# A transformer trunk on one core: where the weight halves, the last pool and some small tiles lie in SBUF, and the order of two groups of small matmuls

## The chip, the core and the metric

The kernel runs on one core of a Trainium2 chip. Its engines run side by side, each through its own queue of instructions: TensorE (PE in the profile; its weight loads are PEld), VectorE (DVE), ScalarE (ACT), GpSimd (POOL) and SyncE (SP), the last of which only issues DMAs here. The metric is the device time of one execution in microseconds (us), and the median of several runs is compared. One core alone is used, so no core waits for another.

## The reference

One layer over a sequence of 256 positions and 2048 channels, all in float32. Cut to what matters:

```python
h = rms_norm(x, norm_g)
proj = h @ w_in                                   # 2048 x 24576
a_qkv, a_gate, b_in, b_gate, c_qkv, c_gate, merge = split(proj)
# A: 3 groups of dilated windowed attention, 8 heads of 128, combined by their denominators
# B: width-3 convolution, then two long FFT convolutions with implicit filters
# C: differential attention, 8 heads, two softmax maps per head, RMSNorm per head
branches = [A * silu(a_gate), B * silu(b_gate), C * silu(c_gate)]
proj_b = einsum('bsnw,nwd->bsnd', branches, w_proj)   # 3 x 1024 x 2048
y = sum(sigmoid(merge + merge_b) * proj_b)
out = rms_norm(x + y @ w_out, final_g)
```

## The kernel before

**The stream of weights.** All weights (`w_in`, `w_proj`, `w_out`) are cut on the host into `NU` = 232 units of 1 MB, [128, 2048] float32 each, in the order in which they are used (`_plan`, L34). Unit i is loaded by SyncE into one of three `raw` buffers (`load`, L167). Each half of a unit (1024 columns) is then split into a high part, rounded to the matmul's short float format (`fp32r`), and the remainder: ScalarE casts the high part (L180), VectorE subtracts (L181). The result is the tile `hl[i, h]`, [128, 2, 1024], with the high part first and the low part 4096 bytes behind it, in four buffers that take turns.

**How a unit is multiplied** (`mm_unit`, L717). A product of two split operands is taken as three matmuls, high·high, high·low and low·high. Two layouts are used.

- Layout b (gates, conv, q and k): the weight half is the stationary operand, 128 columns at a time, and the activations stream: L740 streams 512 elements (high and low activations side by side), L742 streams 256 with the low weight. A half has eight such pairs. In units 0 to 15 the activations are the tiles `xg`, later `hT`.
- Layout a (v, merge, proj, out): the activations are stationary, and the weight half streams in pieces of 512: L761, L762 and L763, 24 matmuls in a unit. The activations are `hT` for v and merge, `bhl` (the split output of a branch) for proj, `yhl` (the split merged output) for out. Every matmul has a weight load of its own, also where two follow each other with the same stationary operand.

**Where tiles lie.** A tile's place is its byte address in each partition. The pools give addresses in the order of allocation, so one tile of odd size moves all that follow. Pieces of `hl`, `hT`, `xg`, `bhl` and `yhl` start at whole multiples of 512 bytes from their tile's start, so a tile's place modulo 512 is that of all its pieces. The built program has:

| tiles | pool or tag | place modulo 512 before |
|---|---|---|
| `hl` (both halves of all units) | `base`, tag `hl` | 288 |
| `hT` | `base` | 288 |
| `xg`, `bhl0`, `bhl2`, `yhl1` to `yhl3`, `qka`, `qkb`, `va`, `vb`, `cv` | `base`, tag `slab` | 256 |
| `bhl1`, `yhl0` | last pool `n`, tag `slab2` | 480 |
| `hidHL`, `dftHL`, `idftHL` (tables of branch B) | `base` | 352 |
| work tiles of branches A and B (`PTh`, `ef`, `vh`, `zh` ...) | pool `ab` | 480 |

**What sets the order.** The program is written out unit by unit (L1009 to L1106): for unit i, the results of unit i-1 are taken out of PSUM, unit i+1 is split, unit i+3 is loaded, and unit i is multiplied in two halves. Between the two halves of a unit stands at most one step of each of two task queues, "a" (attention) and "b" (the rest). Each step issues a short group of other matmuls and the work of VectorE and ScalarE on it. So PE alternates: a half of a unit, a group of small matmuls, a half, and so on. The groups that matter here:

- `t_attn_a` (L525), for each of eight heads: the logits `lg` (twice `mm3`, three matmuls of split operands at L385 to L387, each with 256 elements, and four plain float32 matmuls at L533, each of which PE runs as two passes); one unit later the transposes `pt` (L560, L563); one unit later the product `av` (`mm3`, eight float32 matmuls at L577, `mm3`).
- the forward transforms `ps_f` (L385 to L387, twelve matmuls) and the filters `ps_ef` (L438) of branch B.
- once, in unit 8: `stats_rstd` (L311, two transposes L314, then `std` on ScalarE and `rstd` on VectorE) and `strip_products` (L246, two float32 matmuls L250).

Ahead of everything, 14 float32 matmuls on a tile of ones (L242) run while the first loads are under way. The same tile gives one column to the norm of branch C (L666).

Small tiles (`mx`, `sm`, `rc`, `cmx`, `csm`, `crc`, `ms`, `lam_e`, `tot`, `ss`, `st`, `diff_g`) are allocated where they are first used.

Of the kernel before, what the change touches and what calls it, by code (L numbers as in the profile page):

```python
# [10 lines left out]
F32 = mybir.dt.float32  # L11
F32R = mybir.dt.float32r
# [66 lines left out]
UNITS = _plan()  # L79
# [77 lines left out]
def trunk_kernel(ctx: ExitStack, tc: tile.TileContext, A, out, dbg=None):  # L157
    nc = tc.nc
# [4 lines left out]
    phase = {}  # L163
# [3 lines left out]
    def load(i):  # L167
        if i < NU:
            raw[i] = base.tile([128, 2048], F32, name=f"raw{i}", tag="raw", bufs=3)
            n = 2 if i == 1 else 1  # L170
            for h in range(n):
                c = slice(2048 // n * h, 2048 // n * (h + 1))
                nc.sync.dma_start(raw[i][:, c], A["ws"][i][:, c])

    def split_part(i, h, c):
        if (i, h) not in hl:
            hl[i, h] = base.tile([128, 2, 1024], F32R, name=f"hl{i}_{h}", tag="hl", bufs=4)
        t = hl[i, h][:, :, c]
        src = raw[i][:, 1024 * h:1024 * h + 1024][:, c]
        nc.scalar.copy(t[:, 0], src)  # L180
        nc.vector.tensor_tensor(t[:, 1], src, t[:, 0].bitcast(F32), op=OP.subtract)  # L181
# [11 lines left out]
    def k4(name, shape, dt=F32):  # L193
        return phase["ab"].tile(shape, dt, name=name, tag="k4", bufs=6)
# [43 lines left out]
    tabl = const("tabl", [35, 32])  # L238

    wps = psum.tile([128, 128], F32, name="wps", tag="pa")  # L240
    for j in range(14):
        nc.tensor.matmul(wps, ones, ones, start=j == 0, stop=j == 13)  # L242
    wide_acc = psum.tile([128, 2, 512], F32, name="acc4", tag="pb")
# [13 lines left out]
    dft = slab("dft", [128, 4, 128])  # L257
    idft = base.tile([128, 4, 128], F32, name="idft", tag="i2")
    convw = const("convw", [128, 24, 3])
    diff_g = const("diff_g", [128, 1])  # L260

# [5 lines left out]

    convraw = []
    for j in range(2):
        t = base.tile([128, 260], F32, name=f"convraw{j}")  # L270
        nc.vector.memset(t[:, 0:1], 0.0)
        nc.vector.memset(t[:, 258:260], 0.0)
        convraw.append(t)

# [33 lines left out]

    tot = base.tile([128, 2], F32, name="tot")

# [214 lines left out]
    def t_attn_a(h):  # L525
# [4 lines left out]
        for qt in range(2):  # L530
            mm3(lg[:, qt, 0:256], q(qk, 0, qt), q(qk, 1, qt), qk[:, 2], qk[:, 3], True, True)
            for g in (1, 2):
                nc.tensor.matmul(lg[:, qt, 128 + 128 * g:256 + 128 * g], q(qk2, 2 * g - 2, qt),  # L533
                                 q(qk2, 2 * g - 1, qt), start=True, stop=True)
        P = k4(f"P{h}", [128, 2, 512])
        mx = base.tile([128, 2], F32, name=f"mx{h}", tag="mx", bufs=2)
        sm = base.tile([128, 2], F32, name=f"sm{h}", tag="sm", bufs=2)
        for qt in range(2):
# [3 lines left out]
            else:  # L542
# [6 lines left out]
                                 accum_out=sm[:, qt:qt + 1])  # L549
        rc = base.tile([128, 2], F32, name=f"rc{h}", tag="rc", bufs=2)  # L550
        nc.vector.reciprocal(rc, sm)
# [41 lines left out]
    def lam_init():  # L593
        lamp = k1("lamp").rearrange("p (a d) -> p a d", a=4)
        nc.gpsimd.dma_start(lamp, bass.AP(tensor=A["lamp"].tensor, offset=A["lamp"].offset,
                                          ap=[[0, 128], [64, 4], [1, 64]]))
        pr = k1("lam_p")
        prv = pr[:, 0:128].rearrange("p (a d) -> p a d", a=2)
        lv = lamp.rearrange("p (a b) d -> p a b d", a=2)
        nc.vector.tensor_tensor(prv, lv[:, :, 0], lv[:, :, 1], op=OP.mult)  # L600
        e = base.tile([128, 2], F32, name="lam_e")
        nc.vector.tensor_reduce(e, prv, axis=mybir.AxisListType.X, op=OP.add)
        nc.scalar.activation(e, e, AF.Exp)
        nc.vector.scalar_tensor_tensor(nlam, e[:, 1:2], -(0.8 - 0.6 * math.exp(0.0)), e[:, 0:1],
                                       op0=OP.add, op1=OP.subtract)

    def t_attn_c(h):
# [8 lines left out]
        P = phase["c"].tile([128, 2, 2, 256], F32, name=f"cP{h}", tag="cP", bufs=1)  # L616
        mx = base.tile([128, 4], F32, name=f"cmx{h}", tag="cmx", bufs=2)
        sm = base.tile([128, 4], F32, name=f"csm{h}", tag="csm", bufs=2)
        for qt in range(2):
            bias = cb[:, 1 - qt:3 - qt].rearrange("p s j -> p (s j)")  # L620
            for m in range(2):
# [5 lines left out]
                                     accum_out=sm[:, j:j + 1])  # L627
        rc = base.tile([128, 2, 2], F32, name=f"crc{h}", tag="crc", bufs=2)
        nc.vector.reciprocal(rc, sm.rearrange("p (a b) -> p a b", a=2))
# [27 lines left out]
    def t_cnorm():  # L657
        co = CO["o"]
        ms = base.tile([128, 16], F32, name="ms")
        ps = psum.tile([128, 16], F32, name="ps_ms", tag="pb")  # L660
        prev = None
        for hp in range(5):
            if prev is not None:
                for j in range(4):
                    c = 4 * (hp - 1) + j
                    nc.tensor.matmul(ps[:, c:c + 1], prev[:, j // 2, 128 * (j % 2):128 * (j % 2) + 128],  # L666
                                     ones[:, 0:1], start=True, stop=True)
# [49 lines left out]
    def mm_unit(i, h, ms=(0, 1)):  # L717
        u = UNITS[i]
        t = hl[i, h]
        if i < NS:  # L720
# [288 lines left out]
    for i in range(NU):  # L1009
        if i == i_conv:  # L1010
            load_abias(0)
            load_abias(1)
# [10 lines left out]
        if i == i_n[0] + 18:  # L1023
            drain("a")
            c_ctx.close()
            phase["n"] = n_ctx.enter_context(tc.tile_pool(name="n", bufs=1))
            tasks["b"].append(t_bsplit(1, slab2))
        if i == i_n[1] + 10:
            tasks["b"].append(t_bsplit(2, slab))
        if i == i_out:  # L1030
            for m in range(2):
                xres.append([])
                for j in range(2):
                    t = slab2(f"xres{m}_{j}", [128, 1024])
                    nc.gpsimd.dma_start(t, A["x"][m][:, 1024 * j:1024 * j + 1024])
                    xres[m].append(t)
                fin.setdefault("ss", []).append(base.tile([128, 4], F32, name=f"ss{m}"))
            fin["g"] = []
# [70 lines left out]
    for m in range(2):  # L1109
        st = base.tile([128, 4], F32, name=f"st{m}")  # L1110
        nc.vector.tensor_reduce(st[:, 0:1], fin["ss"][m][:, 0:3], axis=mybir.AxisListType.X, op=OP.add)
# [69 lines left out]
```

## Time and profile before

| | |
|---|---|
| median of 3 runs | 1413.57 us (1412.72 to 1414.65) |
| the profiled execution | 1414.19 us, of which 1412.4 us are the span from the first to the last instruction |
| matmuls and weight loads in it | 7382 each |
| granted TensorE clock | 0.999 of full |
| HBM read | 262.07 MB, 187 GB/s over the span |

How to read it: an instruction is named by its line, engine, operation and tiles, as out<-in without buffer numbers. Matmuls overlap in the records: a matmul of 512 elements is shown with some 0.39 us, yet the next one starts after 0.23 us. What a matmul costs in a dense stream is therefore the distance from one start to the next, not its shown length. The view of windows gives, for a stretch of time, how many instructions of each engine fall in it; a stretch divided by its weight loads is that distance. PE's count in a window has one or two more, since those under way at the edges are counted too.

### The profile page before, as it was taken

How to read it: one execution, taken by the hardware profiler on the slowest of the kernel's cores; microseconds unless marked ns; L12 is line 12 of the kernel's file. 1: busy time of each engine (PE TensorE's matmuls, PEld its weight loads, DVE VectorE, ACT ScalarE, POOL GpSimd, SP SyncE). 2: the span in 40 equal slices, each digit the busy share in tenths (PEclk: the TensorE clock that was granted, in tenths of full speed). 3: DMA queues.
4: the chain of work that ended last, by engine and by line, in shares of the span. 5: the costliest groups of instructions: out<-in, count | busy, mean ns of one | idle time of the engine just before them, and what ended most of it. 6: DMA issues, size and time to landing. Idle time of an engine off the chain costs nothing.

```text
span 1412.4 us, 18607 instructions
## 1 busy us (share of the span) xinstructions
PE 1401.9 (99%) x7382; PEld 1199.7 (85%) x7382; DVE 917.2 (65%) x1245; ACT 702.8 (50%) x1019; POOL 48.7 (3%) x84
## 2 busy tenths in 40 slices
PE   9999999999999999999999999999999999999997
PEld 8888888888988888888888888888888888888886
DVE  5697767676767676576655677765655655555554
ACT  5665544544454444444455675764444444444443
POOL 1000000000000000000000000000000000000000
PEclk9999999999999999999999999999999999999999
DMA  9665555554555544554455555555555555557552
GB/s 343 205 206 200 180 174 173 171 185 168 161 171 185 193 164 159 168 206 150 150 192 187 177 184 173 186 186 187 186 197 205 194 209 191 200 197 276 179 204 94
DMA packets 41943, 265.47 MB, mean 188 GB/s; under 512 B 5619, under 2 KB 5630, under 8 KB 12416
## 3 DMA queue, kind: packets, MB, share of 16 engines
q1 hardware_dynamic: 35712, 246.44, 49.5%
q0 software_dynamic: 5568, 16.80, 4.4%
q8 instruction: 58, 0.95, 0.3%
q10 hardware_dynamic: 576, 1.05, 0.2%
q14 instruction: 29, 0.24, 0.0%
HBM read 262.07 MB, written 2.20 MB: 187 GB/s over the span
## 4 chain that ended last, share of the span: by engine, by line
PE 99%; DMA 0%; DVE 0%; SPq 0%; ACT 0%; issue 0%; DVEq 0%
PE acc L740 28%; PE acc L761 16%; PE acc L762 16%; PE acc L763 16%; PE acc L742 14%; PE acc L728 1%; PE acc L729 1%; PE ps_ef L438 1%; PE ps_o L504 1%; PE av L577 1%; PE lg L533 1%; DMA raw<-in_ws 0%; PE ps_fZ L385 0%; PE clg L615 0%; PE ps_fG L386 0%; PE ps_fZ L386 0%
## 5 line engine op out<-in xcount | busy, mean ns | idle before, releaser
L181 DVE TENSOR_TENSOR hl<-raw,hl 128x1024 fp32r<-128x1024 f32 (+1 forms) x465 | 560.1, 1220 | 220.7 <-ACT hl L180 217.7
L180 ACT CAST hl<-raw 128x1024 fp32r<-128x1024 f32 (+1 forms) x465 | 478.7, 1046 | 244.7 <-PE acc L763 209.6
L740 PE MATMUL acc<-hT,hl 128*128 128x512 f32 x1536 | 542.6, 397 | 0.0
L742 PE MATMUL acc<-hT,hl 128*128 128x256 f32 x1536 | 431.3, 281 | 0.0
L740 PEld LDWEIGHTS acc<-hT,hl 128*128 128x128 f32 x1536 | 288.3, 188 | 65.3 <-issue 0.3
L742 PEld LDWEIGHTS acc<-hT,hl 128*128 128x128 f32 x1536 | 291.0, 189 | 0.5
L761 PE MATMUL acc<-hl,hT 128*128 128x512 f32 x640 | 250.7, 392 | 0.0
L762 PE MATMUL acc<-hl,hT 128*128 128x512 f32 x640 | 249.6, 390 | 0.0
L763 PE MATMUL acc<-hl,hT 128*128 128x512 f32 x640 | 249.6, 390 | 0.0
L763 PEld LDWEIGHTS acc<-hl,hT 128*128 128x128 f32 x640 | 120.2, 188 | 25.0
L762 PEld LDWEIGHTS acc<-hl,hT 128*128 128x128 f32 x640 | 120.3, 188 | 24.3 <-DVE hl L181 0.2
L761 PEld LDWEIGHTS acc<-hl,hT 128*128 128x128 f32 x640 | 120.3, 188 | 24.2
L769 ACT COPY eb<-acc 128x256 f32<-128x256 f32 x80 | 29.6, 372 | 123.7 <-PE acc L742 119.8
L761 PE MATMUL acc<-hl,bhl 128*128 128x512 f32 x192 | 75.9, 395 | 0.0
L762 PE MATMUL acc<-hl,bhl 128*128 128x512 f32 x192 | 75.9, 395 | 0.0
L763 PE MATMUL acc<-hl,bhl 128*128 128x512 f32 x192 | 75.4, 393 | 0.0
L740 PE MATMUL acc<-xg,hl 128*128 128x512 f32 x160 | 56.9, 398 | 0.0
L761 PE MATMUL acc<-hl,yhl 128*128 128x512 f32 x128 | 50.6, 395 | 0.0
L762 PE MATMUL acc<-hl,yhl 128*128 128x512 f32 x128 | 50.6, 395 | 0.0
L763 PE MATMUL acc<-hl,yhl 128*128 128x512 f32 x128 | 50.4, 394 | 0.0
L742 PE MATMUL acc<-xg,hl 128*128 128x256 f32 x160 | 45.1, 282 | 0.0
L763 PEld LDWEIGHTS acc<-hl,bhl 128*128 128x128 f32 x192 | 36.0, 188 | 8.5
(314 smaller groups left out, 1328.0 us busy)
## 6 DMA issues: line engine op xcount, KB each, us to landing
raw<-in_ws SPq DMA_DIRECT2D x230, 1024.0 KB, 4.9
mb<-in_merge_b POOLq DMA_DIRECT2D x12, 256.0 KB, 3.4
xt<-in_xT SPq DMA_DIRECT2D x8, 256.0 KB, 8.0
tok<-in_x POOLq DMA_DIRECT2D x4, 512.0 KB, 10.9
w<-in_w POOLq DMA_DIRECT2D x8, 256.0 KB, 4.7
xres<-in_x POOLq DMA_DIRECT2D x4, 512.0 KB, 7.6
raw<-in_ws SPq DMA_DIRECT2D x3, 512.0 KB, 7.6
ab<-strips POOLq DMA_DIRECT2D x8, 192.0 KB, 3.5
```

What stands on the lines that cost most here:

```text
L180: nc.scalar.copy(t[:, 0], src)
L181: nc.vector.tensor_tensor(t[:, 1], src, t[:, 0].bitcast(F32), op=OP.subtract)
L438: nc.tensor.matmul(ps[:, tt], hidHL[:, 128 * tt:128 * tt + 128], wh[:, j], start=j == 0, stop=j == 1)
L504: nc.tensor.matmul(ps[:, ct, 128 * par:128 * par + 128], p[:, par, f, 128 * ct:128 * ct + 128], idft[:, 2 * par + f], start=f == 0, stop=f ...
L533: nc.tensor.matmul(lg[:, qt, 128 + 128 * g:256 + 128 * g], q(qk2, 2 * g - 2, qt), q(qk2, 2 * g - 1, qt), start=True, stop=True)
L577: nc.tensor.matmul(av[:, qt], v2[:, qt, g - 1, v0:v0 + 128], PTg[:, 2 * g - 2 + qt], start=False, stop=False)
L740: nc.tensor.matmul(acc, t[:, 0, 128 * j:128 * j + 128], m, start=first and j == 0, stop=False)
L742: nc.tensor.matmul(acc[:, 0:256], t[:, 1, 128 * j:128 * j + 128], m[:, 0:256], start=False, stop=last and j == 7)
L761: nc.tensor.matmul(o, xh, wh, start=kt == 0, stop=False)
L762: nc.tensor.matmul(o, xh, wl, start=False, stop=False)
L763: nc.tensor.matmul(o, xl, wh, start=False, stop=kt == u["kt"] - 1)
L769: nc.scalar.copy(t, acc[:, 256:512])
```

## The change

Eight edits, none of which adds or removes a matmul.

1. A tile `hl` becomes 2056 elements wide, 32 bytes more than it needs. A unit's two parts are laid from byte 0 of it or from byte 32 (`halves`): from byte 0 for the units of proj whose branch is not 1 and for the units of out with t > 0; from byte 32 for all others.
2. The four buffers of `hl` get tags of their own, and small tiles are put between them (`put`), with pads, so that each buffer starts at 256 modulo 512.
3. In the last pool, `n`, a tile of 320 bytes (`npad`) is allocated first, and a tile `pad2` of 128 bytes in `base`.
4. The small tiles are allocated once, two of a kind by turns, in the room between the buffers.
5. The tile of ones becomes two: `ones_w` [128, 128] for the matmuls ahead of everything, in a `k1` buffer, and `ones` [128, 1].
6. `convraw` is allocated ahead of `convw`.
7. In `t_attn_a` the float32 matmuls of both query tiles come first, then both `mm3`.
8. In unit 8 `strip_products` comes ahead of `stats_rstd`.

| tiles | place modulo 512 before | after |
|---|---|---|
| `hl` of proj with branch 0 or 2, and of out with t > 0 | 288 | 256 |
| all other `hl` | 288 | 288 |
| `hT` | 288 | 288 |
| `xg`, `bhl0`, `bhl2`, `yhl1` to `yhl3` and the other slabs | 256 | 256 |
| `bhl1`, `yhl0` | 480 | 288 |
| `hidHL`, `dftHL`, `idftHL` | 352 | 320 |
| work tiles in the pools of branches A, B and C | 480 | 480 |

```diff
+    def halves(i, h):
+
+        u = UNITS[i]
+        slabs = u["kind"] == "proj" and u["br"] != 1 or u["kind"] == "out" and u["t"] > 0
+        o = 0 if slabs else 8
+        return hl[i, h][:, o:o + 2048].rearrange("p (a b) -> p a b", a=2)
+
     def split_part(i, h, c):
         if (i, h) not in hl:
-            hl[i, h] = base.tile([128, 2, 1024], F32R, name=f"hl{i}_{h}", tag="hl", bufs=4)
-        t = hl[i, h][:, :, c]
+            hl[i, h] = hl_tile(i, h)
+        t = halves(i, h)[:, :, c]
...
-    ones = base.tile([128, 128], F32, name="ones")
-    nc.vector.memset(ones, 1.0)
...
+    ones_w = base.tile([128, 128], F32, name="ones_w", tag="k1", bufs=8)
+    nc.vector.memset(ones_w, 1.0)
     wps = psum.tile([128, 128], F32, name="wps", tag="pa")
     for j in range(14):
-        nc.tensor.matmul(wps, ones, ones, start=j == 0, stop=j == 13)
+        nc.tensor.matmul(wps, ones_w, ones_w, start=j == 0, stop=j == 13)
...
+    def hl_tile(i, h):
+        return base.tile([128, 2056], F32R, name=f"hl{i}_{h}", tag=f"hl{(2 * i + h) % 4}")
+
+    hl[0, 0] = hl_tile(0, 0)
+    put(*[(f"{k}{j}", n) for k, n in (("mx", 2), ("sm", 2), ("rc", 2), ("cmx", 4), ("csm", 4), ("crc", 4))
+          for j in range(2)], ("lam_e", 2), ("tot", 2), ("ones", 1))
+    hl[0, 1] = hl_tile(0, 1)
+    put(("ms", 16), ("ss0", 4), ("ss1", 4), ("st0", 4), ("st1", 4), ("diff_g", 1), ("pad0", 64))
+    hl[1, 0] = hl_tile(1, 0)
+    put(("pad1", 120))
+    hl[1, 1] = hl_tile(1, 1)
...
         for qt in range(2):
-            mm3(lg[:, qt, 0:256], q(qk, 0, qt), q(qk, 1, qt), qk[:, 2], qk[:, 3], True, True)
             for g in (1, 2):
                 nc.tensor.matmul(lg[:, qt, 128 + 128 * g:256 + 128 * g], q(qk2, 2 * g - 2, qt),
                                  q(qk2, 2 * g - 1, qt), start=True, stop=True)
+        for qt in range(2):
+            mm3(lg[:, qt, 0:256], q(qk, 0, qt), q(qk, 1, qt), qk[:, 2], qk[:, 3], True, True)
...
     def mm_unit(i, h, ms=(0, 1)):
         u = UNITS[i]
-        t = hl[i, h]
+        t = halves(i, h)
...
         if i == i_conv:
+            base.tile([128, 32], F32, name="pad2")
...
             phase["n"] = n_ctx.enter_context(tc.tile_pool(name="n", bufs=1))
+            phase["n"].tile([128, 80], F32, name="npad")
...
         if i == NS + 2:
+            strip_products()
             stats_rstd()
-            strip_products()
```

Two places where instructions move. The first is PE at the logits of head 0, between the two halves of unit 36; `lg` is their output, `qka` and `qkb` the head's queries and keys, and `acc<-hT,hl` the unit's own matmuls. Before:

```order
L742 MATMUL acc_0_2049<-hT,hl_0_1994 128x256
L385 MATMUL lg_2066<-qka_1752 128x256
L386 MATMUL lg_2066<-qka_1752 128x256
L387 MATMUL lg_2066<-qka_1752 128x256
L533 MATMUL lg_2066<-qkb_1753 128x128 x2
L385 MATMUL lg_2066<-qka_1752 128x256
L386 MATMUL lg_2066<-qka_1752 128x256
L387 MATMUL lg_2066<-qka_1752 128x256
L533 MATMUL lg_2066<-qkb_1753 128x128 x2
L740 MATMUL acc_0_2049<-hT,hl_1_1997 128x512
```

After, with the lines of the changed kernel (L411 to L413 are `mm3`, L558 is the float32 matmul):

```order
L769 MATMUL acc_0_2072<-hT,hl_0_2017 128x256
L558 MATMUL lg_2089<-qkb_1776 128x128 x4
L411 MATMUL lg_2089<-qka_1775 128x256
L412 MATMUL lg_2089<-qka_1775 128x256
L413 MATMUL lg_2089<-qka_1775 128x256
L411 MATMUL lg_2089<-qka_1775 128x256
L412 MATMUL lg_2089<-qka_1775 128x256
L413 MATMUL lg_2089<-qka_1775 128x256
L767 MATMUL acc_0_2072<-hT,hl_1_2020 128x512
```

Before, the rows from L385 to L533 stand once for each query tile. Now the group begins with all its float32 matmuls, and the last matmul ahead of the unit's second half is one of `mm3` where it was a float32 one. The seven other heads move alike.

The second place is PE between the halves of unit 8, where `tot` holds the sums of squares and `ps_strip` the products for the position bias. Before:

```order
L740 MATMUL acc_0_572<-xg_131,hl_0_517 128x512
L742 MATMUL acc_0_572<-xg_131,hl_0_517 128x256
L314 MATMUL pst<-ident,tot 128x128 x2
L250 MATMUL ps_strip<-oh,tabl 32x384 x2
L740 MATMUL acc_0_572<-xg_132,hl_1_520 128x512
```

After:

```order
L767 MATMUL acc_0_594<-xg_158,hl_0_539 128x512
L769 MATMUL acc_0_594<-xg_158,hl_0_539 128x256
L257 MATMUL ps_strip<-oh,tabl 32x384 x2
L340 MATMUL pst<-ident,tot 128x128 x2
L767 MATMUL acc_0_594<-xg_159,hl_1_542 128x512
```

The transposes of `tot` now stand behind the strip's matmuls. On DVE only the filling of the tiles of ones moves, at the very start, and becomes two instructions; the queues of ACT, POOL and SP hold what they held, in the same order.

More of the change, by code (lines that the diff above doesn't have):

```diff
@@ L258, in trunk_kernel, with put @@
     idft = base.tile([128, 4, 128], F32, name="idft", tag="i2")
+    convraw = [base.tile([128, 260], F32, name=f"convraw{j}") for j in range(2)]
     convw = const("convw", [128, 24, 3])
-    diff_g = const("diff_g", [128, 1])
+    small = {}
+    def put(*names):
+        for name, n in names:
+            small[name] = base.tile([128, n], F32, name=name)
+    def hl_tile(i, h):
[8 more added lines that the diff above has]
+    hl[1, 1] = hl_tile(1, 1)
+    ones = small["ones"]
+    nc.vector.memset(ones, 1.0)
+    diff_g = small["diff_g"]
     def load_consts():
@@ L266, in load_consts @@
             nc.gpsimd.dma_start(t, A[name])
-    convraw = []
-    for j in range(2):
-        t = base.tile([128, 260], F32, name=f"convraw{j}")
+    for t in convraw:
         nc.vector.memset(t[:, 0:1], 0.0)
         nc.vector.memset(t[:, 258:260], 0.0)
-        convraw.append(t)
     xg = [slab(f"xg{j}", [128, 2, 512], F32R) for j in range(8)]
@@ L307, in stats_square @@
         nc.scalar.activation(tok[j], tok[j], AF.Square, accum_out=sq[:, j // 2, j % 2:j % 2 + 1])
-    tot = base.tile([128, 2], F32, name="tot")
+    tot = small["tot"]
     def stats_rstd():
@@ L549, in t_attn_a @@
                                  accum_out=sm[:, qt:qt + 1])
-        rc = base.tile([128, 2], F32, name=f"rc{h}", tag="rc", bufs=2)
+        rc = small[f"rc{h % 2}"]
         nc.vector.reciprocal(rc, sm)
@@ L600, in lam_init @@
         nc.vector.tensor_tensor(prv, lv[:, :, 0], lv[:, :, 1], op=OP.mult)
-        e = base.tile([128, 2], F32, name="lam_e")
+        e = small["lam_e"]
         nc.vector.tensor_reduce(e, prv, axis=mybir.AxisListType.X, op=OP.add)
@@ L627, in t_attn_c @@
                                      accum_out=sm[:, j:j + 1])
-        rc = base.tile([128, 2, 2], F32, name=f"crc{h}", tag="crc", bufs=2)
+        rc = small[f"crc{h % 2}"].rearrange("p (a b) -> p a b", a=2)
         nc.vector.reciprocal(rc, sm.rearrange("p (a b) -> p a b", a=2))
@@ L658, in t_cnorm @@
         co = CO["o"]
-        ms = base.tile([128, 16], F32, name="ms")
+        ms = small["ms"]
         ps = psum.tile([128, 16], F32, name="ps_ms", tag="pb")
@@ L666, in t_cnorm @@
                     nc.tensor.matmul(ps[:, c:c + 1], prev[:, j // 2, 128 * (j % 2):128 * (j % 2) + 128],
-                                     ones[:, 0:1], start=True, stop=True)
+                                     ones, start=True, stop=True)
             if hp < 4:
@@ L1036, in trunk_kernel @@
                     xres[m].append(t)
-                fin.setdefault("ss", []).append(base.tile([128, 4], F32, name=f"ss{m}"))
+                fin.setdefault("ss", []).append(small[f"ss{m}"])
             fin["g"] = []
@@ L1109, in trunk_kernel @@
     for m in range(2):
-        st = base.tile([128, 4], F32, name=f"st{m}")
+        st = small[f"st{m}"]
         nc.vector.tensor_reduce(st[:, 0:1], fin["ss"][m][:, 0:3], axis=mybir.AxisListType.X, op=OP.add)
```

8 lines of the change are left out of this document (4 added, 4 removed).

## The prediction

> **What bounds the kernel now.** I read the page first: the span, the engines' shares, the granted clock, the chain that ended last.
>
> ```profile
> span 1412.4 us, 18607 instructions
> PE 1401.9 (99%) x7382; PEld 1199.7 (85%) x7382; DVE 917.2 (65%) x1245; ACT 702.8 (50%) x1019; POOL 48.7 (3%) x84
> PEclk9999999999999999999999999999999999999999
> PE 99%; DMA 0%; DVE 0%; SPq 0%; ACT 0%; issue 0%; DVEq 0%
> ```
>
> PE is busy from end to end, at full clock, and is the chain. The view of waits has only three rows for PE, all at the start:
>
> ```profile
> PE wps L242 <- DVE convraw L272: 1.1, 1, 1.1
> PE acc L729 <- DVE hl L181: 0.8, 1, 0.8
> PE acc L728 <- ACT hl L180: 0.7, 1, 0.7
> ```
>
> So the time is 7382 matmuls, each at its distance from the next. A change of this kind can pay only by changing that distance, or lose by making PE wait. I therefore took distances stage by stage. In layout a, stretches that hold nothing but L761 to L763 (first column the stretch in us, then its length, then PE, PEld and the others, with counts):
>
> ```profile
> core 0: us, PE busy (x) PEld busy (x) DVE busy (x) ACT busy (x) POOL busy (x), PEclk, DMA share, GB/s
> 1179.75:1190.63 10.88, 10.88 (x49) 9.02 (x48) 7.89 (x8) 4.20 (x4) 0.00 (x0) 1.00 0.56 197
> 1168.76:1179.75 10.99, 10.99 (x49) 9.03 (x48) 6.10 (x7) 5.14 (x5) 0.54 (x1) 1.00 0.61 211
> 1201.52:1212.71 11.19, 11.19 (x49) 9.01 (x48) 6.13 (x7) 5.14 (x5) 0.54 (x1) 1.00 0.60 216
> 1314.31:1319.81 5.50, 5.50 (x25) 4.51 (x24) 5.43 (x6) 2.10 (x2) 0.00 (x0) 1.00 0.29 100
> 1342.96:1359.74 16.78, 16.78 (x73) 13.52 (x72) 8.88 (x8) 6.09 (x7) 0.00 (x0) 1.00 0.63 224
> ```
>
> These are, in order: merge (stationary `hT`), proj of branch 1 (`bhl1`), proj of branch 2 (`bhl2`), out with t = 0 (`yhl0`), out with t = 1 to 3. Divided by the weight loads, a matmul takes 10.88 / 48 = 226.7 ns with `hT`, 229.0 with `bhl1`, 233.1 with `bhl2`, 229.2 with `yhl0`, 16.78 / 72 = 233.1 with the other `yhl`. The instructions are alike: 128 weights loaded, 512 elements streamed. What differs in the program is the place modulo 512 of what meets: the halves stream from 288 in all of them, and the weights come from 288, 480, 256, 480, 256. The distance follows the place, not the stage: out shows both values within one chunk.
>
> In layout b, a unit's half is eight pairs of L740 and L742; the windows hold whole halves (the first four rows one half each, the last three four halves, 32 pairs):
>
> ```profile
> 231.31:234.15 2.84, 2.84 (x18) 2.47 (x17) 2.77 (x6) 1.32 (x2) 2.16 (x4) 1.00 1.06 224
> 719.81:722.64 2.83, 2.83 (x18) 2.45 (x17) 2.31 (x5) 2.56 (x4) 0.00 (x0) 1.00 0.30 124
> 246.85:249.62 2.77, 2.77 (x18) 2.44 (x17) 1.58 (x3) 2.27 (x3) 0.00 (x0) 1.00 0.48 201
> 733.45:736.22 2.77, 2.77 (x18) 2.44 (x17) 1.58 (x3) 2.51 (x4) 0.00 (x0) 1.00 0.98 324
> 334.67:345.97 11.30, 11.30 (x66) 9.81 (x65) 7.09 (x10) 5.72 (x9) 0.00 (x0) 1.00 0.49 177
> 431.90:443.00 11.10, 11.10 (x66) 9.80 (x65) 7.53 (x11) 5.34 (x9) 0.00 (x0) 1.00 0.54 187
> 31.72:43.02 11.30, 11.30 (x66) 9.82 (x65) 4.68 (x6) 4.49 (x7) 3.79 (x7) 1.00 0.98 334
> ```
>
> Here the same instructions on the same places (`hT` and `hl` both at 288) run at two speeds: 11.30 / 32 = 353 ns a pair, or 11.10 / 32 = 347. The timeline shows that a half keeps the speed of the one before it until a group of small matmuls stands between them, and that the kind of the group decides. The first two rows are the first and the last of 15 halves behind a group of logits, which ends in float32 matmuls: all 15 slow. The next two are the first and the last of 48 behind an `av` group, float32 matmuls and then `mm3`: all 48 fast. Behind the forward transforms 39 of 43 are slow, behind `ps_ef` 6 of 15. The last row is `xg` (at 256): units 0 to 15 settle at 353 whatever stands between.
>
> **The change part by part.** The sum is made against the profiled execution's own 1414.19 us: the span of 1412.4 and 1.8 around it. That run is 0.62 above the median of 1413.57.
>
> Slab stages (edits 1 and 2). The counts of matmuls come from the groups, of which one line of three is
>
> ```profile
> L761 PE MATMUL acc<-hl,bhl 128*128 128x512 f32 x192 | 75.9, 395 | 0.0
> L761 PE MATMUL acc<-hl,yhl 128*128 128x512 f32 x128 | 50.6, 395 | 0.0
> ```
>
> so proj has 3 x 192 = 576, 192 for each branch, and out 3 x 128 = 384, a quarter of them with t = 0. Branches 0 and 2 (384) and out with t > 0 (288) get halves at 256 against weights at 256: 672 matmuls that meet on equal places where they met at a distance of 32. Twelve of them end a run, and load the next unit's weights from 288 while a half streams from 256; these I price as unequal, and they were equal before, so 660 gain and 12 lose 6.4 ns. No row shows 256 against 256 in layout a. The bounds: as fast as the equal places at 288, 226.7, and not below, since no row is faster; at worst both members bring a loss of their own, the weights 6.4 (merge against `bhl2`) and the stream another 6.4 (a pair with `xg` at 256 against a fast one), 239.5. I take 226.7, because the nearest row in kind, equal against equal, has it, and because unequal is slow both ways round (288 on 256, and `xg` 256 on 288). That is 648 x 6.4 ns = **-4.15 us**; at the other end +4.2.
>
> The TensorE page of the Trainium skill ("TensorE: Matmul & The Clock Gate", step by step in Part 2) speaks against any such gain: the streamed operand and the weight load have read ports of their own, so that a load takes nothing from the running matmul. By it the places would not matter and this term would be nil; the windows, 226.7 against 233.1 at full clock, do not agree.
>
> Last pool at 288 (edit 3). `bhl1` and `yhl0` go from 480 to 288, equal to their halves: 192 x 2.3 + 96 x 2.5 ns = **-0.7 us**, bounded by nil and by these rows, since the result is the pair that merge already shows.
>
> Logits (edit 7). The group keeps its matmuls, but ends in `mm3` as `av` does. The rows at head 7, logits and then `av`:
>
> ```profile
> 716.31 0.28 PE L386 MATMUL lg<-qka 128*128 128x256 f32 x1
> 716.43 0.28 PE L387 MATMUL lg<-qka 128*128 128x256 f32 x1
> 716.55 0.61 PE L533 MATMUL lg<-qkb 128*128 128x128 f32 x4
> ...
> 729.43 1.05 PE L577 MATMUL av<-PTg,vb 128*128 128x128 f32 x8
> 730.24 0.37 PE L385 MATMUL av<-PTh,va 128*128 128x256 f32 x1
> 730.44 0.28 PE L386 MATMUL av<-PTh,va 128*128 128x256 f32 x1
> ```
>
> If the 15 halves turn fast, that is 15 x (11.30 - 11.10) / 4 = 0.75, **-0.8 us** with the second switch from float32 saved; if not, nil. I take the gain: 48 of 48 behind the like group are fast. The first work on the logits, on DVE, waits for the whole tile already, so it comes no later. Its row in the tile's view:
>
> ```profile
>   PE lg L533: 4.8, 7
> ```
>
> Strip first (edit 8). `std` waits for four more passes, 1.47 us. ACT and DVE have nothing to do behind it for longer than that:
>
> ```profile
> 57.47 1.47 PE L250 MATMUL ps_strip<-oh,tabl 35*32 35x384 f32 x4
> 57.58 0.48 ACT L316 ACTIVATE std<-pst,eps 128x256 f32<-128x256 f32 x1 [0.77 <-PE pst L314]
> 62.00 0.37 ACT L769 COPY eb<-acc 128x256 f32<-128x256 f32 x1 [3.95 <-PE acc L742]
> 62.41 0.42 DVE L777 TENSOR_TENSOR br<-acc,eb 128x256 f32<-128x256 f32 x1 [2.49 <-ACT eb L769]
> ```
>
> DVE idles 2.49 us and loses 1.47 of it: nil. Without that cover PE could wait for a late `hl` half by at most 1.5 us. The speed behind it is that of `xg`, slow either way.
>
> Ones, tables, pads (edits 2 to 6). The first matmuls on data are held by ACT and DVE, not by the ones:
>
> ```profile
> 10.81 0.19 PEld L728 LDWEIGHTS acc<-xg,hl 128*128 128x128 f32 x1 [1.07 <-ACT hl L180]
> 12.08 0.19 PEld L729 LDWEIGHTS acc<-xg,hl 128*128 128x128 f32 x1 [1.07 <-DVE hl L181]
> ```
>
> so a fill of some 0.1 us more is swallowed there: nil. The tables of branch B go from 352 to 320. That may change the speed behind the forward transforms and behind `ps_ef`: if the 39 slow halves turn fast, -2.0 us; if the 9 fast ones turn slow, +0.5. I take nil, as no row tells, and keep both ends.
>
> Sum: -4.15 - 0.7 - 0.8 = -5.6 us; 1414.19 - 5.6 = 1408.6 for an execution like the profiled one, **1408.0** for the median.
>
> **The rivals.** *Equal at 256 gains nothing.* The weights at 256 are the loss, wherever the halves lie. For it: every row with weights at 256 is slow. Against it: `xg` streams from 256 against weights at 288, and is slow too, so place alone does not say it. Then edits 3 and 7 remain: 1413.57 - 1.5 = 1412.1; with half of the gain 1410.
>
> *The places do nothing.* The stages differ for a reason that the program's places only go along with, such as a load's length from each tile. Against it: `bhl1` and `bhl2` are tiles of one shape filled by one task, and take 229.0 and 233.1. Time: 1413.6, or 1412.8 with the logits. On the SBUF page of the Trainium skill ("SBUF — State Buffer", specifications) lines are 16 bytes long; 256, 288 and 480 are all whole lines, so it would side with this rival, and no run here shows such a line.
>
> *Slower: 256 against 256 costs both losses.* In the slab stages the 660 matmuls go to 239.5 ns, 6.4 more: +4.2. With edit 3 that is 1413.57 + 4.2 - 0.7 = 1417.1, with the logits too 1416.3. It decides from (0.7 + 0.8) / 660 = 2.3 above 233.1 on: beyond 235.4 ns the kernel is slower than before. For it: weights at 256 and streams at 256 are each slow in a row of their own. Against it: both of those rows are unequal places.
>
> *Faster still:* the moved tables turn the halves behind the transforms fast: 1406.0.
>
> **How the numbers follow.** Forecast 0.53 (1407 to 1410, with or without the logits), faster still 0.10, half the gain 0.09, no gain at 256 0.12, places do nothing 0.06, slower 0.10 (0.06 of it beyond 0.2%). A measurement of this kernel tells about 0.2%, 2.8 us, from no change: below 1410.7 is faster, above 1416.4 slower. Faster: 0.53 + 0.10 + half of 0.09, 0.67; slower 0.06; same 0.27. The range 1405.0 to 1413.0 holds the forecast, faster still, half the gain and no gain at 256, 0.84, and leaves out the other two.
>
> **What would show it.** After: stretches of proj and out at 10.9 us for 48 loads, all three branches alike; halves behind the logits at 2.77; PE's waits still three rows. Proj of branches 0 and 2 at 11.19 or above with `bhl1` at 10.88 would show that equal places at 256 are not like those at 288. Logits followed by 2.83 would show that the end of the group does not decide. A new row in PE's waits, at `hl`, would make the whole sum wrong.

## The result, and the profile after

| | before | after |
|---|---|---|
| median, us | 1413.48 (1412.72 to 1414.65, 6 runs) | 1406.72 (1405.79 to 1407.12, 6 runs) |
| profiled execution, us | 1414.19, span 1412.4 | 1406.78, span 1404.9 |

After / before is 0.995, 95% interval 0.994 to 0.996: 6.8 us less, where 5.6 were forecast (1408.0) and the range was 1405.0 to 1413.0.

The page of the changed kernel, with the lines that answer to those of before (span; busy time of each engine; granted clock):

```profile
span 1404.9 us, 18608 instructions
...
PE 1394.1 (99%) x7382; PEld 1197.1 (85%) x7382; DVE 916.6 (65%) x1246; ACT 702.9 (50%) x1019; POOL 49.1 (3%) x84
...
PEclk9999999999999999999999999999999999999999
```

PE is as full as before, at the same clock, with the same 7382 matmuls. The time went out of the distance between them. PE's waits (engine, tile and line that waits, who releases it, total us, times, longest) are still three rows, at the start:

```profile
PE wps L249 <- DVE convraw L299: 1.1, 1, 1.1
PE acc L756 <- DVE hl L188: 1.0, 2, 0.8
PE acc L755 <- ACT hl L187: 0.9, 2, 0.6
```

The groups of proj and out that the prediction counted (L788 was L761; busy us, mean ns of one):

```profile
L788 PE MATMUL acc<-hl,bhl 128*128 128x512 f32 x192 | 75.0, 390 | 0.0
L788 PE MATMUL acc<-hl,yhl 128*128 128x512 f32 x128 | 50.0, 390 | 0.0
```

They say only that a mean got 5 ns shorter. Where, the windows say (stretch in us, its length, then PE, PEld and the others):

```profile
1164.32:1175.20 10.88, 10.88 (x50) 9.01 (x49) 6.09 (x7) 5.14 (x5) 0.54 (x1) 1.00 0.64 215
1175.20:1186.08 10.88, 10.88 (x50) 9.01 (x49) 7.88 (x8) 4.20 (x4) 0.00 (x0) 1.00 0.56 197
1196.97:1207.88 10.91, 10.91 (x50) 9.01 (x49) 6.09 (x7) 5.15 (x5) 0.54 (x1) 1.00 0.64 221
1308.72:1314.19 5.47, 5.47 (x25) 4.50 (x24) 5.43 (x6) 2.10 (x2) 0.00 (x0) 1.00 0.25 99
1336.91:1353.27 16.36, 16.36 (x74) 13.52 (x73) 8.90 (x8) 6.14 (x7) 0.00 (x0) 1.00 0.65 227
230.78:233.56 2.78, 2.78 (x19) 2.45 (x17) 2.71 (x6) 1.33 (x2) 2.20 (x4) 1.00 1.05 224
333.76:344.86 11.10, 11.10 (x67) 9.79 (x66) 7.09 (x10) 5.63 (x9) 0.00 (x0) 1.00 0.50 178
137.29:1395.55 1258.26, 1258.26 (x6633) 1081.60 (x6631) 811.75 (x1073) 619.20 (x882) 34.51 (x56) 1.00 0.53 183
```

The first five are proj of branch 1, merge, proj of branch 2, out with t = 0, out with t = 1 to 3. Counted by their matmuls in the program (48, 48, 48, 24, 72; a window's count can hold one of a neighbour), all five now take 226.7 to 228 ns, where branch 2 and out with t over 0 took 233.1. The sixth is the second half behind the logits of head 0: 2.84 before, 2.78 now. The seventh was forecast to stay: four halves of units 53 and 54, 11.30 before and 11.10 now. They stand behind a group of branch B in unit 52; by the timeline that is the inverse transform (`ps_i`, which reads `idftHL`), which the prediction counted with the forward ones.

The last row is used for every kernel below. It runs from the first matmul of unit 22 to the first one of the last half of all (unit 231, rows 128 to 255), and I call it **the trunk**. The same stretch of the kernel before:

```profile
137.81:1402.95 1265.14, 1265.14 (x6632) 1082.83 (x6631) 812.50 (x1072) 619.13 (x882) 34.44 (x56) 1.00 0.53 182
```

The trunk is 6.88 us shorter. What lies ahead of it varies by more than a microsecond between executions; the trunk does not. A second profile of the unaltered changed kernel, taken later:

> The changed kernel once more, unaltered, beside the next two on one chip, and for a second profile of its start. Theory (the speed of units 1 to 8 falls out at the start, by when the first halves arrive, and differs from execution to execution of one program; from unit 16 on the profile repeats itself): units 8 to 15 at 353.3 again, every later half at the speed that it had in the first profile, units 1 to 8 at either speed, 1405.2 to 1407.2 with 1406.7 the likeliest. Rival (the start too belongs to the program): units 1 to 8 at 353.3 again.

```profile
20.56:54.48 33.92, 33.92 (x195) 29.47 (x194) 20.07 (x27) 20.63 (x32) 8.78 (x16) 1.00 0.83 301
137.87:1396.15 1258.28, 1258.28 (x6633) 1081.89 (x6632) 812.12 (x1073) 619.18 (x882) 34.45 (x56) 1.00 0.53 183
```

1258.28 against 1258.26: profiles of one trunk agree within 0.02 us. So an effect of some tenths can be read there, though the whole times (1405.64 to 1407.35 in these five runs, median 1406.51) scatter by more than one. In the first row, twelve halves of units 2 to 7 take 33.92 / 96 = 353.3 ns a pair, as in the first profile, so this run alone does not tell its two theories apart; later ones do. The half microsecond that unit 22 came earlier in the first profile of after (137.29 against 137.81 before) is not the change's: here it comes at 137.87.

### The profile page after: what moved, and what is told of

Read it like the earlier page. It is cut to its first block, busy times and chain, and to the rows that moved or that the text cites. A ratio compares the mean times of both kernels' runs of the same rounds, so it can differ in the third digit from the quotient of the medians.

```text
span 1404.9 us, 18608 instructions
## 1 busy us (share of the span) xinstructions
PE 1394.1 (99%) x7382; PEld 1197.1 (85%) x7382; DVE 916.6 (65%) x1246; ACT 702.9 (50%) x1019; POOL 49.1 (3%) x84
## 4 chain that ended last, share of the span: by engine, by line
PE 99%; DMA 0%; DVE 0%; SPq 0%; ACT 0%; issue 0%; DVEq 0%
PE acc L767 28%; PE acc L788 16%; PE acc L790 16%; PE acc L789 16%; PE acc L769 14%; PE acc L755 1%; PE acc L756 1%; PE ps_ef L464 1%; PE ps_o L530 1%; PE lg L558 1%; PE av L604 1%; DMA raw<-in_ws 0%; PE ps_fZ L413 0%; PE clg L642 0%; PE clg L641 0%; PE ps_fZ L411 0%
## 5 line engine op out<-in xcount | busy, mean ns | idle before, releaser
L788 PE MATMUL acc<-hl,hT 128*128 128x512 f32 x640 | 250.6, 391 | 0.0
L788 PEld LDWEIGHTS acc<-hl,hT 128*128 128x128 f32 x640 | 120.2, 188 | 24.2
L788 PE MATMUL acc<-hl,bhl 128*128 128x512 f32 x192 | 75.0, 390 | 0.0
L788 PE MATMUL acc<-hl,yhl 128*128 128x512 f32 x128 | 50.0, 390 | 0.0
```

Of the source, the lines that this page charges most:

```text
L788: nc.tensor.matmul(o, xh, wh, start=kt == 0, stop=False)
```

## The experiments

### Four parts undone, one at a time

**The halves from byte 32 again.** Tiles, sizes and buffers stay as changed.

```diff
-        o = 0 if slabs else 8
+        o = 8
```

> The changed kernel with the halves used from byte 32 everywhere; their tiles, sizes and buffers stay as changed. Theory (what counts is whether streamed halves and loaded weights stand on the same place modulo 512): proj of branches 0 and 2 and out with t over 0 go back from 226.7 to 233.1 ns a matmul, a stretch of 48 loads in proj of branch 2 from 10.90 to 11.19 us, proj of branch 1 stays at 10.88; 660 x 6.4 ns less the 12 border matmuls is +4.1 us, 1410.8. Rival (the gain came with the halves' new tiles, each a buffer of its own, and not with the place): all stretches stay at 10.9, 1406.7.

Measured: 1410.74 us (1409.45 to 1412.98), ratio to before 0.9983, interval 0.9974 to 0.9992. Windows of proj of branch 1, proj of branch 2, out with t = 1 to 3, and the trunk:

```profile
1167.23:1178.11 10.88, 10.88 (x50) 9.01 (x48) 6.09 (x7) 5.14 (x5) 0.54 (x1) 1.00 0.65 218
1199.88:1211.07 11.19, 11.19 (x50) 8.99 (x48) 6.14 (x7) 5.14 (x5) 0.54 (x1) 1.00 0.66 218
1341.22:1358.01 16.79, 16.79 (x74) 13.49 (x72) 8.90 (x8) 6.14 (x7) 0.00 (x0) 1.00 0.62 223
139.22:1401.10 1261.88, 1261.88 (x6633) 1081.32 (x6631) 812.32 (x1073) 619.00 (x882) 34.44 (x56) 1.00 0.53 183
```

Branch 2 is back at 11.19, out at 16.79 / 72 = 233.2 ns, and branch 1 has not moved. Thirty-two bytes alone carry it: 1261.88 - 1258.26 = 3.62 us. The rival, that the new tiles and buffers brought the gain, falls.

**The tables of branch B at 352 again.**

```diff
+    base.tile([128, 8], F32, name="pad3")
     hidHL = base.tile([128, 256], F32R, name="hidHL")
...
-            base.tile([128, 32], F32, name="pad2")
+            base.tile([128, 24], F32, name="pad2")
```

> The changed kernel with the three tables of branch B (hidHL, dftHL, idftHL) back from 320 to 352 modulo 512, by 32 bytes of padding ahead of them and 32 fewer behind; nothing else moves. Theory (the place of the tables decides at which speed the layout-b halves run behind the forward transforms): some 39 halves go from 347 to 353 ns a pair, 39 x 8 x 6.67 ns = +2.1 us, less up to 0.5 for the halves behind ps_ef that turn fast, so 1408.3 to 1408.8. Rival (those halves turned fast for another reason, such as the speed that they inherit from the halves ahead): no change, 1406.7.

Measured: 1408.99 us (1407.77 to 1409.29), ratio 0.9963, interval 0.9951 to 0.9976. The four halves of units 53 and 54, and the trunk:

```profile
334.28:345.58 11.30, 11.30 (x66) 9.80 (x65) 7.10 (x10) 5.72 (x9) 0.00 (x0) 1.00 0.48 169
137.60:1397.80 1260.20, 1260.20 (x6632) 1081.81 (x6631) 812.25 (x1072) 619.24 (x882) 34.45 (x56) 1.00 0.53 183
```

They are at 353 ns a pair again. By the timeline so are all 39 halves behind the transforms that read these tables, 27 behind the forward ones (`ps_fG`, `ps_fZ`) and 12 behind the inverse one (`ps_i`); in the changed kernel all 39 are at 347. The trunk is 1.94 us longer. The move of the tables, which the prediction put at nil, is worth 1.9 us. The 39 halves alone make 1.95 of it, and the rest cancels: four halves behind `ps_o`, which reads none of the moved tables, turned slow as well (0.20), while the units of v, in layout a, got 0.28 back.

The start times in the traces show what the two values are. At 353, two pairs of some 350 ns and one of some 361 take turns; at 347, every pair takes 346 or 347.

**The logits in the old order.** Places stay as changed.

```diff
         for qt in range(2):
+            mm3(lg[:, qt, 0:256], q(qk, 0, qt), q(qk, 1, qt), qk[:, 2], qk[:, 3], True, True)
             for g in (1, 2):
                 nc.tensor.matmul(lg[:, qt, 128 + 128 * g:256 + 128 * g], ...
-        for qt in range(2):
-            mm3(lg[:, qt, 0:256], q(qk, 0, qt), q(qk, 1, qt), qk[:, 2], qk[:, 3], True, True)
```

> The changed kernel with the logits' products back in the old order, so that a group ends in float32 matmuls; places stay as changed. Theory (the last matmuls of a group set the speed behind it): 15 halves behind the logits go from 347 to 353 ns a pair, +0.8 us, and the first half behind each group is 0.13 longer again (+1.0 for 8), while the eight groups are 0.09 shorter each (-0.7): net +1.1, 1407.8. Rival (the order inside the group moves time only from the group into the half behind it): the halves stay at 347 and the net is within 0.3 of nil, 1406.4 to 1407.0.

Measured: 1408.01 us (1407.13 to 1408.84), ratio 0.9958, interval 0.9945 to 0.9970. The second half behind the logits of head 0, the group of head 1 itself, and the trunk:

```profile
232.07:234.91 2.84, 2.84 (x19) 2.46 (x18) 2.77 (x6) 1.32 (x2) 2.16 (x4) 1.00 1.07 209
269.37:270.89 1.52, 1.52 (x16) 1.52 (x15) 1.52 (x2) 0.18 (x1) 0.00 (x0) 1.00 0.00 0
138.54:1397.65 1259.11, 1259.11 (x6632) 1081.85 (x6631) 812.08 (x1073) 619.25 (x882) 34.44 (x56) 1.00 0.53 183
```

The group of head 1 in the changed kernel:

```profile
268.03:269.64 1.61, 1.61 (x17) 1.61 (x16) 1.61 (x2) 0.18 (x1) 0.00 (x0) 1.00 0.00 0
```

With the old order the group is 0.09 shorter, and all 15 halves behind the logits are slow; the trunk is 0.85 longer, where the theory had 1.1. The group's row alone would have called the new order a loss of 8 x 0.09 = 0.7 us. The half behind it gains more than that: its first matmul comes sooner and its pairs are 6.7 ns shorter. The rival, which left those halves at 347, falls.

**The last pool at 480 again.**

```diff
-            phase["n"].tile([128, 80], F32, name="npad")
+            phase["n"].tile([128, 128], F32, name="npad")
```

> The changed kernel with the last pool at 480 modulo 512 again; nothing else moves. Theory (places): stretches of proj of branch 1 and of out with t = 0 go from 226.7 to 229 ns a matmul, +0.6 to 0.7 us, 1407.3, and no other stretch moves. Rival (their gain came from elsewhere in the change): no change, 1406.7.

Measured: 1407.23 us (1406.21 to 1407.63), ratio 0.9953, interval 0.9939 to 0.9967. Twelve halves of units 2 to 7, proj of branch 1, the trunk:

```profile
19.66:52.94 33.28, 33.28 (x195) 29.25 (x193) 19.93 (x26) 20.53 (x32) 8.55 (x16) 1.00 0.84 311
1163.61:1174.60 10.99, 10.99 (x50) 9.01 (x48) 6.10 (x7) 5.14 (x5) 0.54 (x1) 1.00 0.60 212
136.26:1394.98 1258.72, 1258.72 (x6633) 1081.56 (x6632) 812.05 (x1073) 619.21 (x882) 34.43 (x56) 1.00 0.53 183
```

Branch 1 is back at 10.99, and the trunk is 0.46 longer. The first row is a surprise: nothing that these twelve halves touch was edited, yet they ran at 33.28 / 96 = 346.7 ns a pair instead of 353.3.

The four undone parts add up to 3.62 + 1.94 + 0.85 + 0.46 = 6.87 us of trunk, and the whole change to 6.88. Nothing of the trunk is left for the other edits or for an interplay.

### Which places are equal

The first half of each merge unit with t = 1 is read from another place, chunk by chunk; the weights `hT` stay at 288. The diff is cut: the buffer that holds these halves is also made 480 bytes longer, in place of the pad behind it, so that nothing else moves.

```diff
+MERGE_AT = [8, 0, 16, 24, 32, 40, 56, 72, 104, 120, 128, 12]
...
+        if u["kind"] == "merge" and u["t"] == 1 and h == 0:
+            o = MERGE_AT[4 * u["br"] + u["ch"]]
```

> The changed kernel, with the first half of each merge unit with t = 1 (24 matmuls a chunk) used from another place in its tile: modulo 512 from 288, 256, 320, 352 in the chunks of branch 0, from 384, 416, 480, 32 in those of branch 1, from 160, 224, 256 (512 bytes further than the first 256) and 304 in those of branch 2, against the weights hT at 288 in all twelve. Theory (what counts is where the streamed half stands against the weights, modulo 512): 226.7 ns a matmul at 288, 233.1 at both 256, about 229 at 480, the others somewhere from 226.7 to 233.1; in all 24 x 11 x up to 6.4 ns, up to 1.7 us more than the changed kernel. Rival A (only the place of the weights counts): all twelve at 226.7. Rival B (the distance in bytes counts, not its rest modulo 512): the second 256 unlike the first.

Such a half holds 12 matmuls, not the 24 that the expectation counted, so its bound halves to 0.85 us. Measured, in one run: 1408.17 us; the trunk is 1259.11, 0.85 longer. Five of the twelve windows, with the half at 256, 320, 352, 480 and 32:

```profile
946.99:949.79 2.80, 2.80 (x14) 2.26 (x13) 1.25 (x2) 2.60 (x4) 0.00 (x0) 1.00 0.82 325
984.38:987.18 2.80, 2.80 (x14) 2.20 (x12) 1.97 (x3) 1.05 (x1) 0.00 (x0) 1.00 0.33 132
1018.08:1020.84 2.76, 2.76 (x13) 2.25 (x12) 1.48 (x2) 1.57 (x2) 0.00 (x0) 1.00 0.61 258
1116.38:1119.18 2.80, 2.80 (x14) 2.25 (x13) 2.11 (x3) 1.57 (x2) 0.00 (x0) 1.00 0.82 319
1149.12:1151.84 2.72, 2.72 (x14) 2.25 (x12) 1.23 (x1) 1.05 (x1) 0.00 (x0) 1.00 0.85 337
```

Divided by 12, that is 233.3, 233.3, 230.0, 233.3 and 226.7 ns. All of them, by how far the half stands behind the weights, modulo 256:

| behind the weights, bytes modulo 256 | 0 (at 32) | 16 | 32 | 64 | 96 | 128 (416, 160) | 192 (480, 224) | 224 (256, and 512 further) |
|---|---|---|---|---|---|---|---|---|
| us for 12 matmuls | 2.72 | 2.77 | 2.80 | 2.76 | 2.81 | 2.79, 2.79 | 2.80, 2.80 | 2.80, 2.79 |

The half left at 288 stands behind a small group and does not give a clean value; halves at 288 elsewhere in this stage take 2.72. Theory against rivals: A falls (the weights stood still), and so does B (the two at 256 agree). But the theory's period was too long: 32 is as good as 288, so places are equal when they agree modulo **256**. The 229.0 ns of `bhl1` at 480 fits as well: a half at 288 stands 64 behind it modulo 256.

The TensorE page of the Trainium skill ("TensorE: Matmul & The Clock Gate", step by step in Part 2) gives the streamed operand and the weight load a read port each, so that the load would take nothing from the matmul. Here like matmuls on one buffer, with only the start address changed, take 226.7 or 233.3 ns. What the two share in the hardware no run shows.

### The tables at a third place

```diff
-    put(("pad1", 120))
+    put(("pad1", 112), ("sq", 4))
...
-    sq = base.tile([128, 2, 2], F32, name="sq")
+    sq = small["sq"].rearrange("p (a b) -> p a b", a=2)
...
-            base.tile([128, 32], F32, name="pad2")
+            base.tile([128, 40], F32, name="pad2")
```

> The changed kernel with the tables of branch B at 288 modulo 512 instead of 320, equal to the halves and hT; nothing else that TensorE reads moves. Theory (the place of a group's operands decides the speed behind it, and 352 gave slow and 320 fast behind the forward transforms): behind the transforms, behind ps_ef and behind the inverse transform each group gives one speed throughout; if all turn fast, the 9 halves that are slow behind ps_ef in the changed kernel gain 0.4 us, 1406.3; if the transforms turn slow, +2.1, 1408.8. Rival (the tables act only through 352, all other places being alike): as the changed kernel, 1406.7.

Measured: 1408.64 us (1408.13 to 1410.11), ratio 0.9966, interval 0.9954 to 0.9979. Twelve halves of units 2 to 7, the four of units 53 and 54, the trunk:

```profile
22.48:55.76 33.28, 33.28 (x195) 29.25 (x193) 18.52 (x24) 19.71 (x31) 8.63 (x16) 1.00 0.78 283
335.77:347.07 11.30, 11.30 (x66) 9.81 (x65) 7.09 (x10) 5.73 (x9) 0.00 (x0) 1.00 0.48 175
139.14:1398.91 1259.77, 1259.77 (x6632) 1081.46 (x6631) 811.93 (x1072) 619.31 (x882) 34.47 (x56) 1.00 0.53 183
```

The trunk is 1.51 us longer, though the tables now stand where halves and `hT` stand. By the timeline 31 of the 39 halves behind the transforms are slow and 8 fast, all 8 behind `ps_fG`: the time came near the theory's second case, but its claim of one speed throughout fell, and so did the rival. For a small group, "equal to the halves" is not the rule: 320 is good, 352 and 288 are not.

### A small group added

```diff
+    def kick(o, a, b):
+        mm3(o, a[:, 0:128], a[:, 256:384], b[:, 0:256], b[:, 256:512], True, True)
...
+        if i == 1:
+            kick(ps_k, xg[0][:, 0], xg[0][:, 1])
...
+        kick(pst[:, 256:512], xg[0][:, 0], xg[0][:, 1])
...
+        kick(ps2[:, 256:512], hT[:, 0], hT[:, 1])
```

> The changed kernel with a group of three F32R matmuls added (128 weights, 256 columns, results not used) at three places: behind the first half of unit 1 (operands xg, at 256), behind the strip products and the transposes of the norm at about 57 us (xg), and behind the second product of the hidden layer at about 104 us (hT, at 288). Theory (a small group sets the speed of the layout-b halves behind it, and one that ends in F32R products on equal places sets it fast): 15 halves of units 1 to 8, 14 of units 8 to 15 up to the next small group, and 10 of units 16 to 21 at 346.7 instead of 353.3, 39 x 53 ns = -2.1 us, for 3 x 0.36 = +1.1 us of added matmuls: 1405.7. Rival (the speed there belongs to the operands of the halves): 353.3 in all of them, and 1407.8.

Measured: 1408.22 us (1407.77 to 1409.78), ratio 0.9964, interval 0.9951 to 0.9976. Behind the first and behind the third added group:

```profile
21.46:55.38 33.92, 33.92 (x194) 29.46 (x193) 19.24 (x24) 19.82 (x32) 9.22 (x16) 1.00 0.82 293
110.32:132.94 22.62, 22.62 (x130) 19.60 (x129) 17.53 (x27) 12.43 (x20) 0.00 (x0) 1.00 0.52 185
```

33.92 / 96 and 22.62 / 64 are both 353 ns, and behind the second group it is the same. The trunk (1258.32) is untouched; a group takes 0.36 to 0.46 us, and no half behind one is fast. So ending in `mm3` is not enough to make a group good, though the logits and `av` had gone that way.

### Equal places in the first units, and at the borders

Units 0 to 15 read `xg` at 256 with halves at 288. Here the halves go to 256.

```diff
-        slabs = u["kind"] == "proj" and ...
+        slabs = u["kind"] == "gate" and u["br"] < 2 or u["kind"] == "proj" and ...
```

> The changed kernel with units 0 to 15 used from byte 0 as well, so that the weights hl and the streamed xg both stand at 256 modulo 512 (before: 288 and 256). Theory (equal places help in layout b as in layout a): the 30 halves of units 1 to 15 go from 353 to 347 ns a pair, 30 x 8 x 6.67 ns = -1.6 us, 1405.1. Rival (in layout b the speed is set by how the stretch was entered, at the start and behind each small group, and the place does not matter): both speeds can be seen, changing at the groups at 56, 95 and 104 us, and the time is 1405.1 to 1406.8 as the start falls out. In the run with the pool at 480, which has the same places up to there as the changed kernel, units 1 to 8 ran at 346.7 with unequal places, which speaks for the rival.

Measured: 1407.22 us (1405.03 to 1408.11, 4 runs), ratio 0.9951, interval 0.9935 to 0.9966. Units 2 to 7, units 9 to 13 (behind the strip products), and the trunk:

```profile
22.47:55.75 33.28, 33.28 (x195) 29.34 (x193) 18.49 (x24) 19.73 (x31) 8.59 (x16) 1.00 0.78 283
63.07:90.80 27.73, 27.73 (x162) 24.26 (x161) 25.52 (x47) 20.59 (x36) 4.03 (x6) 1.00 0.63 195
137.93:1396.21 1258.28, 1258.28 (x6633) 1081.63 (x6631) 811.83 (x1073) 619.35 (x882) 34.45 (x56) 1.00 0.53 183
```

Both stretches are at 346.7 ns. That looks like the theory. The same program beside the unaltered kernel:

> The kernel with units 0 to 15 used from byte 0 (both at 256) once more, beside the unaltered one. Theory (equal places with xg make the halves behind the strip products and behind the hidden layer fast, as its first profile shows: 13 and 9 halves more than in the changed kernel, while the start falls out by chance): 22 x 53 ns = 1.2 us below the unaltered kernel of the same call, some 1405.5. Rival (what these halves gain the start loses again: its first halves arrived 2.5 us later in the first profile): the same as the unaltered kernel within 0.3.

Measured: 1406.66 us (1405.19 to 1409.43) against 1406.51 for the unaltered kernel beside it; ratio 0.9941, interval 0.9928 to 0.9955. The same three windows:

```profile
22.77:56.70 33.93, 33.93 (x195) 29.42 (x194) 18.30 (x24) 19.74 (x31) 8.38 (x16) 1.00 0.77 273
64.10:92.37 28.27, 28.27 (x163) 24.54 (x161) 26.07 (x47) 21.14 (x37) 4.03 (x6) 1.00 0.62 192
139.97:1398.24 1258.27, 1258.27 (x6633) 1081.88 (x6631) 812.10 (x1073) 619.17 (x882) 34.44 (x56) 1.00 0.53 183
```

One program, two profiles: 346.7 in one, 353.3 in the other, in the same halves. So in layout b equal places do not set the speed; a stretch is entered in one of two ways and stays in it. Which one it is at the start falls out by the execution. (The two come from different chips. The run below is the same program up to unit 30, was taken on the chip of the second, and shows 346.7 again, so the chip does not explain it.) The two profiles also show what the small group at 57 to 61 us does: with equal places each speed was carried through it. With `xg` unequal it was not: units 9 to 13 are at 353.3 in all ten such profiles, though units 2 to 7 came in at 346.7 in two of them (pool at 480, tables at 288). The theory's 1.2 us falls; there is no gain in the median.

The last run adds the first halves behind a border from layout a to layout b.

```diff
+        enters = i > 0 and h == 0 and u["lay"] == "b" and UNITS[i - 1]["lay"] == "a"
-        o = 0 if slabs else 8
+        o = 0 if slabs or enters else 8
```

> As the one before, and the first half of each layout-b unit that follows a layout-a unit (units 30, 52, 78, 100, 124, 136) is used from byte 0 too, at 256 against hT at 288. In every profile so far the halves behind such a border, up to the next small group, run at 353.3: 16 of them. Theory (the speed is a phase in which the stretch is entered, and a stretch entered on unequal places can come out in the fast one): up to 10 of the 16 turn fast, -0.5 us against the one before. Rival (a border gives the slow speed whatever the first half's place): no difference, within 0.1 in those stretches.

Measured: 1406.80 us (1406.50 to 1407.90), ratio 0.9947, interval 0.9935 to 0.9960. Units 2 to 7, the four halves of units 53 and 54, and the trunk:

```profile
21.11:54.38 33.27, 33.27 (x194) 29.36 (x193) 19.65 (x26) 20.27 (x32) 9.17 (x16) 1.00 0.82 294
333.06:344.36 11.30, 11.30 (x67) 9.81 (x66) 7.09 (x10) 5.73 (x9) 0.00 (x0) 1.00 0.51 176
136.57:1395.61 1259.04, 1259.04 (x6633) 1081.88 (x6631) 812.50 (x1073) 619.18 (x882) 34.44 (x56) 1.00 0.53 183
```

Five of the six moved halves turned fast (that of unit 136 was so before), the second halves of units 30, 78 and 124 stayed slow, and the trunk is 0.77 us **longer** than with equal places in the first units alone: 17 of the 39 halves behind the transforms, whose own groups were not edited, turned slow, all 12 behind `ps_i` among them. Neither theory nor rival had that. So what a group leaves behind depends on what comes into it.

No version here beats the changed kernel.

## Why the prediction was right

The forecast's main mechanism held: equal places at 256 run as equal places at 288 do. The sum came out 1.2 us short. That is the net of two terms sized 0.8 us too large together and one, the tables, put at nil that was worth 1.94. So the measured 1406.7 lies inside the range but just below the forecast's own band of 1407 to 1410, on the side of the rival *faster still*. By its own terms, each measured by undoing it (trunk):

| term | forecast, us | measured, us |
|---|---|---|
| slab stages | -4.15 | -3.62 |
| last pool at 288 | -0.7 | -0.46 |
| logits | -0.8 | -0.85 |
| tables of branch B | nil (-2.0 to +0.5) | -1.94 |
| sum | -5.6 | -6.87 |

- **Slab stages.** Right in kind: moving only the halves back restores 233.1 ns. The size was 0.5 too large. A run of equal places is not at its steady distance from the first matmul: the first half of a run behind a border averages some 229 ns, so that a stretch of branch 2 takes 10.91 and not 10.88. By the start times the excess is gone after some ten matmuls. The runs of merge and of out with t = 0 that follow a slab run start in the same way. The prediction priced one matmul at each of 12 borders.
- **Last pool.** Right in kind. Branch 1 gave its 4 x 0.11; out with t = 0 gave a third of its share or less, as each of its runs now follows a border too (5.47 us for 24, not 5.44).
- **Logits.** Right to 0.05 us of trunk, and all 15 halves turned. But the time is the net of a loss in the group (+0.7) and a larger gain behind it, where the prediction expected a little to be saved inside it. And its reason, that a group ending in `mm3` leaves a fast half behind, is no general rule: the added groups ended so and left slow ones.
- **Tables.** Here is the error. The prediction bounded this edit at -2.0 and took nil "as no row tells". The end of the bound came true, so the rival *faster still* (1406.0, chance 0.10) happened on top of the forecast. All rows of before have the tables at 352, so none could tell the sign; the runs show 352 slow, 320 fast, 288 mostly slow. The gain is real, but where the tables landed decided it, and that it came on top of the forecast was luck. Its reading of the rows, 39 slow halves of 43 behind the forward transforms, was not right either. By the start times before, 27 halves stand behind those and 12 behind the inverse one, and all 39 are slow.
- **Strip first, ones, pads at nil.** Not contradicted. They act ahead of the trunk, where unit 22 begins between 136.3 and 140.0 us over all profiles, so nothing below a microsecond can be read there.

Of the rivals, *equal at 256 gains nothing*, *the places do nothing* and *256 against 256 costs both losses* fell with the windows of proj and out. One support of the forecast fell with them: "unequal is slow both ways round" rested in part on `xg` at 256, and units 2 to 7 have since run at 346.7 with unequal places. In layout a the equality rule was tested directly and holds; in layout b it was only read into the rows, and one program with equal places ran there at both speeds. That the kind of a small group decides the speed behind it fell too, as a general rule: the place of its tables changed that speed, and so did what ran ahead of it.

## What to carry to other kernels

Where PE is full at full clock and like instructions take unlike times, compare the start addresses of what streams and of the weights loaded, modulo 256: 32 bytes were worth 6.4 ns of 233 for a matmul of the slab stages here. When a kernel has that much reproducible length and a start that is not, compare a fixed stretch of two profiles rather than medians; it resolved 0.02 us where whole times scatter by 1 to 2. And when an edit moves tiles that it does not speak of, price what they feed by both bounds and say which of the two the sum leaves out.

## What the runs showed of the hardware

- For matmuls of 512 columns with a weight load each, in layout a, the distance goes with the place of the stream against the weights modulo 256: 226.7 ns at equal places, 229 to 231 at 16 and 64 behind, 232 to 234 at the others tried. At equal places a run that starts slower comes to 226.7 by itself: by the start times in proj of branch 2 after the change, the first 12 matmuls of a run took 2.745 us, the next 12 took 2.720.
- A pair of matmuls of 512 and 256 columns (layout b) has two speeds, 346.7 and 353.3 ns, on the same addresses; a stretch keeps the one that it was entered with. From unit 22 on the choice was the same in both profiles of each of the two programs that were profiled twice, while at the start it differed between the two profiles of one of them, which is worth 33.93 - 33.28 = 0.65 us over twelve halves.
- What a small group does to that speed depends on its operands' places and on what ran ahead of it. That what is entered is a phase of some kind is an inference from the persistence and from the pairs of 350, 350 and 361 ns that take turns in a slow stretch; no run here shows it directly.
- A matmul of 512 columns took 226.7 ns at best. The Trainium skill gives N / 2.4 + 2.5 ns for N columns at full clock as the gap of an isolated matmul ("TensorE: Matmul & The Clock Gate", back-to-back issue gap in Part 2), from which 215.8 ns would be the estimate. The granted clock was 1.00 in every window above, so the measurement is 11 ns above that. No run here shows what takes them.
